# Bringing the solves' inverses back by 6 transfers instead of 12, with another split of heads over partitions

## The chip, the core and the metric

The kernel runs on one core of one Trainium2 chip. The metric is device time in microseconds (us) of one execution; lower is better.

## What is computed

The reference is one layer of a hybrid decoder. 256 tokens of width 2048 are normalised and projected once; half of the projected columns feed a sparse attention with 8 heads, the other half an RWKV-7 mixer with 16 heads of 64; both results are gated, projected out, normalised and added to the input. The change lies in the RWKV-7 part, whose core in the reference is a recurrence over tokens:

```python
def step(state, inp):
    r_t, w_t, k_t, v_t, a_t, b_t = inp
    sa = jnp.einsum('bhij,bhj->bhi', state, a_t)
    state = (state * w_t[:, :, None, :] + sa[..., None] * b_t[:, :, None, :]
             + v_t[..., None] * k_t[:, :, None, :])
    return state, jnp.einsum('bhij,bhj->bhi', state, r_t)
```

## The kernel before, in words

TensorE (PE) does almost all of the work: the input projection as a stream of weight tiles. A weight tile of 128 x 1024 (512 KB) is loaded by the SP queue into a raw buffer `rf__N` (line 281; four buffers), split by ScalarE (ACT) into a high part `hf__N` (line 289) and by VectorE (DVE) into a low part `lf__N` (line 290, called a cast here; three buffers), and multiplied with the activations `xH` and `xL` in 24 matmuls of 256 columns: 16 with `hf`, then 8 with `lf`. The last tiles of the stream, `ht`, `lt` and `ho`, `lo`, are of the same kind.

The rest of the layer is written as Python generators in "lanes". A planner steps them between the projection's pieces and gives each instruction a priority; from that, a scheduler puts every engine's instructions into one fixed order. At run time each engine follows its order and waits where an input is not there yet, so an instruction that waits holds up all that stands behind it on its engine.

The RWKV-7 recurrence is done in chunks of 64 tokens, in two halves of 8 heads (`hb` 0 and 1). For each half, `solve` (line 715) inverts 32 triangular 64 x 64 systems (8 heads, 4 chunks), each as two 32 x 32 diagonal blocks and one off-diagonal block:

1. Four transfers (line 726) take the diagonal blocks from the tile `GR` to a DRAM scratch `us`, and one (line 732) brings them back as 64 systems on 64 partitions, in `U`.
2. 62 VectorE instructions (lines 739 and 741) build the 64 inverses in `Z`, and line 744 copies the transposed inverses to `U`.
3. `Z` goes to the DRAM scratch `zs`, `U` to `zt` (lines 747 and 748, 256 KB each).
4. Eight transfers of 32 KB (line 761) bring the inverses back into the tile `ZB`, and four (line 768) the transposed ones of the first diagonal block into `ZT`. In traces both tiles are called `arena`, after the memory that they lie in; they are told apart by their source, `zs` or `zt`. Their runs of consecutive bytes are one row of 32 numbers, 128 bytes.
5. PE multiplies `GR` with `ZT` (32 matmuls of 32 x 32, lines 772 to 778; the first product from here on), VectorE copies it out (line 784), PE multiplies that with `ZB` (32 more, lines 789 to 796; the second product), and VectorE copies the off-diagonal blocks into `ZB` (line 799). A float32 matmul counts as two instructions in the profile.
6. The chunk loop (lines 808 to 884) runs four chunks one after the other through PE, ACT, VectorE and GpSimd (POOL).

A half has four feature tiles `i` of two heads each. Before, tile `i` worked on partition half `i % 2` in the steps 4 to 6; `i // 2` chose the columns there. This is why a read of one partition block needs tiles 0 and 2, or 1 and 3, which lie apart in the scratch, and takes two transfers:

```python
for a in range(2):
    SP.dma_start(ZBv[b0:b0 + 32, a, :, 32 * d:32 * d + 32], zsv[d, mp, :, a])
```

Of the kernel before, what the change touches and what calls it, by code (L numbers as in the profile page):

```python
# [16 lines left out]
P = 128  # L17
# [104 lines left out]
def hybrid_block(ctx: ExitStack, tc: tile.TileContext, xT, xtok, wfm, wtm, wout, vecs, gpost, lora, table,  # L122
                 onehot, consts, pos, cw1, cw2, out):
    nc = tc.nc
    PE, DVE, ACT, POOL, SP = nc.tensor, nc.vector, nc.scalar, nc.gpsimd, nc.sync
# [589 lines left out]
    def solve(hb):  # L715
# [3 lines left out]
        GR, AR, VS, KT, PC = A.GR, A.AR, A.VS, A.KT, A.PC  # L719
# [3 lines left out]
        for par in range(2):  # L723
            for d in range(2):
                b0 = 64 * (1 - par) + 32 * d
# [4 lines left out]
        U = Us.ap.rearrange("p (s t) -> p s t", s=32)[0:64]  # L730
# [13 lines left out]
        DVE.tensor_copy(U, Z.rearrange("p s t -> p t s"))  # L744
        zs = dp.tile([64, 32, 32], F32, tag="zs", name=f"zs{hb}")
        zt = dp.tile([64, 32, 32], F32, tag="zt", name=f"zt{hb}")
        SP.dma_start(zs, Z)
        SP.dma_start(zt, U)
        Us.free(3.0)
        Zs.free(3.0)  # L750
        ZBs = yield from sb(4)
        ZB = ZBs.ap.rearrange("p (j t) -> p j t", j=16)
        for mp in range(2):
            POOL.memset(ZB[64 * mp + 32:64 * mp + 64, :, 0:32], 0.0)
        zsv = zs.rearrange("(d a b k) s t -> d b s a k t", d=2, a=2, b=2)
        ZBv = ZB.rearrange("p (a k) t -> p a k t", a=2)
        for mp in range(2):
            for d in range(2):
                b0 = 64 * mp + 32 * d
                for a in range(2):  # L760
                    SP.dma_start(ZBv[b0:b0 + 32, a, :, 32 * d:32 * d + 32], zsv[d, mp, :, a])
        ZTs = yield from sb(2)
        ZT = ZTs.ap.rearrange("p (h a s) -> p h a s", h=8, a=2)
        ztv = zt.rearrange("(d h a b) t s -> d b t h a s", d=2, h=8, a=2)
        for par in range(2):
            b0 = 64 * (1 - par)
            for a in range(2):
                SP.dma_start(ZT[b0:b0 + 32, :, a, :], ztv[0, par, :, :, a])
        yield 11.0
        t2p = yield from bank2()  # L770
        t2v = t2p[:, :, 0:T].rearrange("p b (j a s) -> p b j a s", j=4, a=2)
        for i in range(4):
            for hh in range(2):
                for c in range(4):
                    b0 = 64 * (1 - c % 2)
                    q0 = 64 * (i % 2) + 32
                    mm(t2v[q0:q0 + 32, c % 2, 2 * (i // 2) + hh, c // 2, :], GR[b0:b0 + 32, i, hh, c, 32:64],
                       ZT[b0:b0 + 32, 2 * i + hh, c // 2, :], start=True, stop=True)
        t2s = yield from sb(2)
# [6 lines left out]
        ZTs.free(1.0)  # L786
        yield 2.0
        zbp = yield from bank()
        for i in range(4):
            for hh in range(2):  # L790
                for c in range(4):
                    q = 2 * (i // 2) + hh
                    j = 4 * q + c
                    q0 = 64 * (i % 2)
                    mm(zbp[q0:q0 + 32, j * 32:j * 32 + 32], t2[q0 + 32:q0 + 64, q, c // 2, c % 2, :],
                       ZB[q0 + 32:q0 + 64, j, 32:64], start=True, stop=True)
        for mp in range(2):
# [10 lines left out]
        for c in range(4):  # L808
            ko = 64 * (c % 2)
            bo = 64 - ko  # L810
            gps = yield from bank()
            for i in range(4):
                q0 = 64 * (i % 2)
                o_ = gps[q0:q0 + 64, (i // 2) * P:(i // 2) * P + P]
                for hh in range(2):
                    s = slice(64 * hh, 64 * hh + 64)
                    mm(o_[:, s], GR[:, i, hh, c, 0:64], VS[:, i, c, s], start=i < 2 and hh == 0,
                       stop=c == 0 and i >= 2 and hh == 1)
            if c:
                for i in range(4):  # L820
                    q0 = 64 * (i % 2)
                    o_ = gps[q0:q0 + 64, (i // 2) * P:(i // 2) * P + P]
                    mm(o_, AR[:, i, c, 0, :], SB.ap.rearrange("p (m t) -> p m t", m=4)[:, i, :], start=False,
                       stop=i >= 2)
            G = yield from sb()
            ACT.activation(G[:], gps[:, :T], AF.Copy)
            gps.free(2.0)
            yield GLAT
            sap = yield from bank2()
            for i in range(4):  # L830
                q0 = 64 * (i % 2)
                for hh in range(2):
                    o = (i // 2) * P + 64 * hh
                    mm(sap[bo:bo + 64, i % 2, o:o + 64], ZB[q0:q0 + 64, 8 * (i // 2) + 4 * hh + c, :],
                       G[q0:q0 + 64, o:o + 64], start=True, stop=True)
            DVE.tensor_copy(VS[bo:bo + 64, :, c, :].rearrange("p (a b) t -> p b a t", b=2),
                            sap[bo:bo + 64, :, 0:T].rearrange("p b (a t) -> p b a t", a=2))
            sap.free(2.0)
            G.free(1.0)
            yield GLAT  # L840
            SBo = SB
            if c < 3:
                sp = yield from bank()
                for i in range(4):
                    for hh in range(2):
                        s = slice(64 * hh, 64 * hh + 64)
                        mm(sp[s, i * 64:i * 64 + 64], KT[:, i, c, s], VS[:, i, c, s], start=True, stop=True)
                pcb = PC[:, :, c:c + 1].to_broadcast([P, 4, 64])
                S2 = yield from sb()
                S2v = S2.ap.rearrange("p (m t) -> p m t", m=4)  # L850
                spv = sp[:, :T].rearrange("p (m t) -> p m t", m=4)
                if c:
                    DVE.tensor_tensor(S2v, spv, SC.ap.rearrange("p (m t) -> p m t", m=4), op=ALU.add)
                    SC.free(1.0)
                else:
                    DVE.tensor_copy(S2v, spv)
# [12 lines left out]
            for i in range(4):  # L869
                o_ = yp[64 * (i % 2):64 * (i % 2) + 64, (i // 2) * P:(i // 2) * P + P]  # L870
                for hh in range(2):
                    s = slice(64 * hh, 64 * hh + 64)
                    mm(o_[:, s], GR[:, i, hh, c, 64:128], VS[:, i, c, s], start=i < 2 and hh == 0,
                       stop=c == 0 and i >= 2 and hh == 1)
            if c:
                for i in range(4):
                    o_ = yp[64 * (i % 2):64 * (i % 2) + 64, (i // 2) * P:(i // 2) * P + P]
                    mm(o_, AR[:, i, c, 1, :], SBo.ap.rearrange("p (m t) -> p m t", m=4)[:, i, :], start=False,
                       stop=i >= 2)
# [19 lines left out]
        for a in range(2):  # L899

            ytp = yield from bank()
            for c in range(4):
                o = T * c + P * a
                transpose(ytp[:, P * c:P * c + P], ysb[:, o:o + P], ident)
            ytv = ytp.ap.rearrange("p (c b t) -> p c b t", c=4, b=2)
            for b in range(2):
                m = 4 * hb + 2 * a + b
                mv = mix[1][:, m, :].rearrange("p (c t) -> p c t", c=4)
                DVE.scalar_tensor_tensor(mv, ytv[:, :, b, :], vcol(V_LNW, m), mv, op0=ALU.mult, op1=ALU.add)
            ytp.free(2.0)  # L910
            yield 0.5
# [493 lines left out]
```

## Time and profile before

| What | us |
|---|---|
| median of three runs | 571.77 |
| lowest and highest of them | 570.47, 571.91 |
| the profiled execution's own time | 571.67 |
| its span, from first to last instruction | 569.9 |
| PE busy in the span | 552.9 |
| VectorE busy | 427.1 |
| ScalarE busy | 311.1 |
| GpSimd busy | 56.3 |

The rows further down come from that one profiled execution, and their times count from the start of its span; 1.77 us of its own time lie outside the span. A matmul's duration in a row includes its pipeline, so matmuls overlap: what one costs in a stream is the distance of two starts.

### The profile page before, as it was taken

The numbers are of one execution on the slowest core, as the hardware profiler recorded it, in microseconds if no ns is written. First come the engines' busy times: TensorE is split into PE (matmuls) and PEld (weight loads), VectorE is DVE, ScalarE is ACT, GpSimd is POOL, SyncE is SP. The second block draws the span as 40 slices with busy tenths as digits, with TensorE's granted clock in tenths as the row PEclk, the third lists the DMA queues.
The fourth block names the chain that finished last, engine by engine and source line by source line (L and its number), as shares of the span: only waits on it lengthen the run. The fifth ranks groups of instructions, "written<-read, shape, count | busy, mean of one in ns | idle before, by whom it ended". The sixth has DMA issues, their size and how long they took to land.

```text
span 569.9 us, 12187 instructions
## 1 busy us (share of the span) xinstructions
PE 552.9 (97%) x4796; PEld 519.1 (91%) x4796; DVE 427.1 (75%) x892; ACT 311.1 (55%) x566; POOL 56.3 (10%) x95
## 2 busy tenths in 40 slices
PE   8999999999899989999999999999999999999994
PEld 8999999989899979999999999999999987778883
DVE  6888998866989955555798969998866664468755
ACT  6858864723346442332878856865633344465532
POOL 3101410510000000000402200000000010000002
PEclk9999999999999997999999999999999999999997
DMA  8857453578745572432364355344574436675623
GB/s 300 363 195 261 156 182 118 183 225 241 248 149 185 188 213 94 154 108 80 106 216 157 101 160 176 96 144 150 165 200 143 154 113 178 229 270 174 217 78 147
DMA packets 41364, 99.95 MB, mean 175 GB/s; under 512 B 14395, under 2 KB 17116, under 8 KB 40924
## 3 DMA queue, kind: packets, MB, share of 16 engines
q1 hardware_dynamic: 41020, 98.88, 53.4%
q8 instruction: 37, 0.61, 0.5%
q10 hardware_dynamic: 288, 0.31, 0.2%
q14 instruction: 19, 0.16, 0.1%
HBM read 93.93 MB, written 5.24 MB: 174 GB/s over the span
## 4 chain that ended last, share of the span: by engine, by line
PE 86%; DMA 5%; DVE 4%; ACT 2%; issue 1%; POOL 1%; SPq 1%; DVEq 0%; ACTq 0%; POOLq 0%
PE banks L156 84%; PE banks L169 2%; DMA arena<-zt 1%; DMA arena<-in_cw_dram 1%; DMA arena<-us 1%; DMA us<-GR 1%; DMA xr<-in_xT_dram 1%; POOL arena L629 1%; DVE y L1302 0%; DMA arena<-zs 0%; DVE arena L950 0%; SPq L726 0%; DVE arena L739 0%; DVE arena L631 0%; POOL arena L630 0%
## 5 line engine op out<-in xcount | busy, mean ns | idle before, releaser
L156 PE MATMUL banks<-arena 128*32 128x128 f32 (+3 forms) x470 | 30.4, 252 | 2.9 <-DMA arena<-in_cw_dram 1.8
L156 PEld LDWEIGHTS banks<-arena 128*32 128x32 f32 (+3 forms) x470 | 26.0, 135 | 6.4 <-DMA arena<-in_cw_dram 2.3
L739 DVE TENSOR_TENSOR arena<-arena 64x31 f32<-64x31 f32 (+15 forms) x62 | 20.4, 330 | 3.0 <-DMA arena<-us 2.4
L741 DVE TENSOR_TENSOR arena<-arena 64x31 f32<-64x31 f32 (+15 forms) x62 | 20.4, 329 | 0.5
L629 POOL TENSOR_SCALAR arena<-arena,small 128x256 f32<-128x256 f32 x8 | 9.6, 1196 | 92.0 <-ACT arena L627 91.7
L541 ACT ACTIVATE small<-small 128x256 f32<-128x256 f32 x25 | 12.3, 499 | 9.3 <-DVE small L539 9.3
L169 PE MATMUL banks<-small,arena 128*128 128x128 f32 x96 | 15.8, 275 | 0.8 <-DVE arena L656 0.5
L542 DVE SCALAR_TENSOR_TENSOR arena<-small 128x256 f32<-128x256 f32 x25 | 12.2, 491 | 4.1 <-ACT small L541 4.0
L156 PE MATMUL banks<-AR,arena 64*128 64x128 f32 x128 | 14.9, 287 | 0.3 <-ACT KT L665 0.3
L156 PEld LDWEIGHTS banks<-AR,arena 64*128 64x128 f32 x128 | 12.1, 187 | 2.5 <-issue 1.5
L596 DVE RECIPROCAL arena<-arena 128x256 f32<-128x256 f32 x8 | 13.8, 1736 | 0.5 <-ACT arena L593 0.5
L1049 ACT ACTIVATE arena<-arena,mx 128x256 f32<-128x256 f32 (+1 forms) x32 | 14.1, 443 | 0.0
L1107 ACT ACTIVATE arena<-arena 128x256 f32<-128x256 f32 x16 | 6.6, 412 | 13.0 <-DVE arena L1221 8.4
L169 PEld LDWEIGHTS banks<-small,arena 128*128 128x128 f32 x96 | 11.3, 140 | 1.9 <-DVE arena L656 0.7
L689 DVE TENSOR_TENSOR GR<-banks,small 128x1024 f32<-128x1024 f32 x8 | 9.8, 1221 | 3.4 <-ACT small L541 1.7
L1306 POOL TENSOR_TENSOR y<-y,xres 128x512 f32<-128x512 f32 x2 | 2.9, 1456 | 94.3 <-ACT y L1305 94.3
L156 PE MATMUL banks<-VS,GR 128*64 128x64 f32 x256 | 11.4, 228 | 0.0
L156 PEld LDWEIGHTS banks<-VS,GR 128*64 128x64 f32 x256 | 9.5, 137 | 2.0 <-DVE mixA L1119 0.4
L539 DVE TENSOR_TENSOR small<-banks,small 128x256 f32<-128x256 f32 x25 | 10.2, 414 | 0.1
L1045 DVE CUSTOM_DVE_ANT_0 arena<-banks,arena 128x256 f32<-128x256 f32 (+1 forms) x32 | 10.1, 348 | 0.0
L862 POOL MEMSET arena<- 64x256 f32 x12 | 3.7, 308 | 64.6 <-DVE arena L1108 36.5
L626 POOL TENSOR_SCALAR arena<-arena 128x256 f32<-128x256 f32 x8 | 8.1, 1013 | 17.6 <-ACT arena L625 17.5
(1375 smaller groups left out, 2148.1 us busy)
## 6 DMA issues: line engine op xcount, KB each, us to landing
arena<-in_cw_dram SPq DMA_DIRECT2D x8, 512.0 KB, 5.3
arena<-in_wfm_dram SPq DMA_DIRECT2D x4, 512.0 KB, 9.4
xres<-in_xtok_dram SPq DMA_DIRECT2D x2, 1024.0 KB, 6.4
xr<-in_xT_dram SPq DMA_DIRECT2D x3, 512.0 KB, 6.8
bscr<-arena SPq DMA_DIRECT2D x1, 1536.0 KB, 6.0
out_dram<-y SPq DMA_DIRECT2D x5, 256.0 KB, 2.3
arena<-bscr SPq DMA_DIRECT2D x8, 128.0 KB, 3.0
gpt<-in_gpost_dram SPq DMA_DIRECT2D x1, 1024.0 KB, 6.4
```

Of the source, the lines that this page charges most:

```text
L156: last[0] = PE.matmul(o, lhsT, rhs, **kw)
L169: PE.transpose(out=o, in_=i, identity=idn)
L539: DVE.tensor_tensor(f[:, 1:T + 1], pt[:, :T], rbc, op=ALU.mult)
L541: ACT.activation(tm, f[:, 0:T], AF.Copy, scale=vcol(V_MU, c))
L542: DVE.scalar_tensor_tensor(o, f[:, 1:T + 1], omu[:, c:c + 1], tm, op0=ALU.mult, op1=ALU.add)
L596: pace(DVE.reciprocal(A.nrm[i + j], A.nrm[i + j]))
L629: POOL.tensor_scalar(fk[:], ta[:], ka2[:, m:m + 1], ka1[:, m:m + 1], op0=ALU.mult, op1=ALU.add)
L689: DVE.tensor_tensor(A.GR[:, i].rearrange("p h c t -> p (h c) t"), gp.ap.rearrange("p h (c t) -> p (h c) t", c=4), gmask[:, None, :].to_bro ...
L739: DVE.tensor_tensor(t_, U[:, 0:j, j:j + 1].to_broadcast([64, j, w]), Z[:, j:j + 1, j:32].to_broadcast([64, j, w]), op=ALU.mult)
L741: DVE.tensor_tensor(Z[:, 0:j, j:32], Z[:, 0:j, j:32], t_, op=ALU.add)
L1045: DVE.tensor_tensor_reduce(out=dst, in0=src, in1=bb, scale=1.0, scalar=-3.0e38, op0=ALU.add, op1=ALU.max, accum_out=mx[:, i, j:j + 1])
L1049: ACT.activation(dst, dst, AF.Exp, bias=mx[:, i, j:j + 1], accum_out=sm[:, i, j:j + 1])
```

## The change

It does three things. The transposed inverses are written to DRAM first in the source, and their reads stand ahead of the others' in it. Feature tile `i` now works on partition half `i // 2`, and `i % 2` chooses the columns, so that a partition block's tiles lie side by side in the scratch: each pair of reads becomes one of 64 KB (four for `ZB`, two for `ZT`). The PE loops go over `i` in the order 0, 2, 1, 3, so that they alternate between partition halves as before; what is computed is the same. Lines after 770 have numbers that are smaller by 3 in the changed kernel.

```diff
+        SP.dma_start(zt, U)
         SP.dma_start(zs, Z)
-        SP.dma_start(zt, U)
         Us.free(3.0)
         Zs.free(3.0)
+        ZTs = yield from sb(2)
+        ZT = ZTs.ap.rearrange("p (h a s) -> p h a s", h=8, a=2)
+        ztv = zt.rearrange("(d r b) t s -> d b t r s", d=2, b=2)
+        for par in range(2):
+            b0 = 64 * (1 - par)
+            SP.dma_start(ZTs[b0:b0 + 32, :].rearrange("p (r s) -> p r s", r=16), ztv[0, par])
         ZBs = yield from sb(4)
         ZB = ZBs.ap.rearrange("p (j t) -> p j t", j=16)
...
-        zsv = zs.rearrange("(d a b k) s t -> d b s a k t", d=2, a=2, b=2)
-        ZBv = ZB.rearrange("p (a k) t -> p a k t", a=2)
+        zsv = zs.rearrange("(d b k) s t -> d b s k t", d=2, b=2)
         for mp in range(2):
             for d in range(2):
                 b0 = 64 * mp + 32 * d
-                for a in range(2):
-                    SP.dma_start(ZBv[b0:b0 + 32, a, :, 32 * d:32 * d + 32], zsv[d, mp, :, a])
-        ZTs = yield from sb(2)
-        ZT = ZTs.ap.rearrange("p (h a s) -> p h a s", h=8, a=2)
-        ztv = zt.rearrange("(d h a b) t s -> d b t h a s", d=2, h=8, a=2)
-        for par in range(2):
-            b0 = 64 * (1 - par)
-            for a in range(2):
-                SP.dma_start(ZT[b0:b0 + 32, :, a, :], ztv[0, par, :, :, a])
+                SP.dma_start(ZB[b0:b0 + 32, :, 32 * d:32 * d + 32], zsv[d, mp])
         yield 11.0
         t2p = yield from bank2()
         t2v = t2p[:, :, 0:T].rearrange("p b (j a s) -> p b j a s", j=4, a=2)
-        for i in range(4):
+        for i in (0, 2, 1, 3):
             for hh in range(2):
                 for c in range(4):
                     b0 = 64 * (1 - c % 2)
-                    q0 = 64 * (i % 2) + 32
-                    mm(t2v[q0:q0 + 32, c % 2, 2 * (i // 2) + hh, c // 2, :], GR[b0:b0 + 32, i, hh, c, 32:64],
+                    q0 = 64 * (i // 2) + 32
+                    mm(t2v[q0:q0 + 32, c % 2, 2 * (i % 2) + hh, c // 2, :], GR[b0:b0 + 32, i, hh, c, 32:64],
                        ZT[b0:b0 + 32, 2 * i + hh, c // 2, :], start=True, stop=True)
...
-            DVE.tensor_copy(VS[bo:bo + 64, :, c, :].rearrange("p (a b) t -> p b a t", b=2),
+            DVE.tensor_copy(VS[bo:bo + 64, :, c, :].rearrange("p (b a) t -> p b a t", b=2),
                             sap[bo:bo + 64, :, 0:T].rearrange("p b (a t) -> p b a t", a=2))
...
-                m = 4 * hb + 2 * a + b
+                m = 4 * hb + 2 * b + a
```

The other loops over `i` in the chunk loop are changed in the same way.

The scheduler makes a new order of it, which differs first in half 0's solve. On PE, in half 0 (the tile `GR_742` is half 0's), the first product's 32 matmuls stood inside the tile `hf__2436`; the row with `arena,GR_742` is that product, the one with `arena` alone the second.

```order
 L156 MATMUL banks<-xH,hf__2369 128x256
 L156 MATMUL banks<-xL,hf__2369 128x256
-L156 MATMUL banks<-xH,lf__2368 128x256 x8
+L156 MATMUL banks<-xH,lf__2368 128x256 x6
+L156 MATMUL banks<-arena,GR_742 32x32 x32
+L156 MATMUL banks<-xH,lf__2368 128x256 x2
 L156 MATMUL banks<-xH,hf__2404 128x256
```

```order
 L156 MATMUL banks<-xH,hf__2436 128x256
+L156 MATMUL banks<-arena 32x32 x32
 L156 MATMUL banks<-xL,hf__2436 128x256
 L156 MATMUL banks<-xH,hf__2436 128x256
-L156 MATMUL banks<-arena,GR_742 32x32
 L156 MATMUL banks<-xL,hf__2436 128x256
-L156 MATMUL banks<-arena,GR_742 32x32 x31
```

The first product now stands 35 projection matmuls earlier, behind the sixth matmul with `lf__2368`. The second product stands 36 earlier than it did (it stood inside `lf__2470`).

On the SP queue, the same place in half 0, before:

```order
L747 DMA zs_2531<-arena 64x1024
L748 DMA zt_2532<-arena 64x1024
L281 DMA rf__2500<-in_wfm_dram 128x1024
L761 DMA arena<-zs_2531 32x8x32 x4
L281 DMA rf__2552<-in_wfm_dram 128x1024
L761 DMA arena<-zs_2531 32x8x32 x4
L281 DMA rf__2582<-in_wfm_dram 128x1024
L768 DMA arena<-zt_2532 32x8x32 x4
```

and in the changed kernel, where `rf__2546` and `rf__2576` are the loads that were called `rf__2552` and `rf__2582`:

```order
L748 DMA zs_2531<-arena 64x1024
L747 DMA zt_2532<-arena 64x1024
L281 DMA rf__2500<-in_wfm_dram 128x1024
L765 DMA arena<-zs_2531 32x16x32 x2
L756 DMA arena<-zt_2532 32x16x32 x2
L281 DMA rf__2546<-in_wfm_dram 128x1024
L765 DMA arena<-zs_2531 32x16x32 x2
L281 DMA rf__2576<-in_wfm_dram 128x1024
```

The scheduler still writes `zs` first and puts two reads of `zs` ahead of the reads of `zt`; but no weight load stands between those and the reads of `zt` any more, where there were two.

On the SP queue in half 1, before:

```order
L747 DMA zs_5233<-arena 64x1024
L281 DMA rf__5202<-in_wfm_dram 128x1024
L748 DMA zt_5234<-arena 64x1024
L281 DMA rf__5253<-in_wfm_dram 128x1024
L761 DMA arena<-zs_5233 32x8x32 x8
L281 DMA rf__5284<-in_wfm_dram 128x1024
L768 DMA arena<-zt_5234 32x8x32 x4
```

and in the changed kernel, where `rf__5163`, `rf__5196`, `rf__5241` and `rf__5272` are the loads that were called `rf__5169`, `rf__5202`, `rf__5253` and `rf__5284`:

```order
L748 DMA zs_5227<-arena 64x1024
L747 DMA zt_5228<-arena 64x1024
L281 DMA rf__5163<-in_wfm_dram 128x1024
L756 DMA arena<-zt_5228 32x16x32 x2
L281 DMA rf__5196<-in_wfm_dram 128x1024
L281 DMA rf__5241<-in_wfm_dram 128x1024
L281 DMA rf__5272<-in_wfm_dram 128x1024
L765 DMA arena<-zs_5227 32x16x32 x4
```

Here the reads of `zt` come first, and the reads of `zs` now stand behind the load that they stood ahead of.

## Rows read from the trace of the kernel before

**Rows 1.** The page, busy time of the engines over the span.

```profile
PE 552.9 (97%) x4796; PEld 519.1 (91%) x4796; DVE 427.1 (75%) x892; ACT 311.1 (55%) x566; POOL 56.3 (10%) x95
```

**Rows 2.** Waits of PE: engine, line, awaited; us in total, times, longest.

```profile
PE banks L156 <- DMA arena<-zt: 2.8, 1, 2.8
PE banks L156 <- DMA arena<-in_cw_dram: 1.8, 2, 1.5
```

**Rows 3.** The chain that ended last, in order of time: start, us, what.

```profile
207.80 5.40 DMA arena<-zt
213.25 76.41 PE banks L156 x880
```

**Rows 4.** Stretches: length, then busy us by engine, granted clock, DMA share, GB/s.

```profile
210.46:213.25 2.79, 0.00 (x1) 0.01 (x1) 0.94 (x2) 0.51 (x1) 0.00 (x0) 0.88 1.02 237
213.25:221.20 7.95, 7.95 (x98) 7.52 (x98) 3.23 (x6) 1.20 (x2) 0.00 (x0) 0.61 0.24 82
423.15:428.64 5.49, 5.49 (x99) 5.15 (x98) 3.27 (x7) 1.28 (x2) 0.00 (x0) 1.00 0.50 159
```

**Rows 5.** The same view, around PE's wait for in_cw_dram.

```profile
145.00:150.00 5.00, 3.78 (x56) 3.37 (x54) 4.90 (x12) 1.93 (x4) 1.03 (x2) 1.00 0.82 275
```

**Rows 6.** Timeline of the SP queue in half 0: start, us, queue, line, transfer.

```profile
198.59 0.46 SPq L748 DMA_DIRECT2D zt<-arena  x1
...
202.54 1.81 SPq L761 DMA_DIRECT2D arena<-zs  x4
204.45 0.39 SPq L281 DMA_DIRECT2D rf__2552<-in_wfm_dram  x1
...
207.80 1.91 SPq L768 DMA_DIRECT2D arena<-zt  x4
```

**Rows 7.** DMA issues by stretch, 197 to 210 us: KB each, median us to landing.

```profile
zt<-arena SPq DMA_DIRECT2D x1, 256.0 KB, 4.5
...
arena<-zs SPq DMA_DIRECT2D x4, 32.0 KB, 2.0
...
arena<-zs SPq DMA_DIRECT2D x4, 32.0 KB, 3.6
...
arena<-zt SPq DMA_DIRECT2D x4, 32.0 KB, 4.9
```

**Rows 8.** Line 726 (the 64 KB transfers us<-GR, both halves): issue to landing.

```profile
DMA to landing us min/median/max: 1.7/1.9/5.3
```

**Rows 9.** Timeline of PE in half 0: start, us, matmul, count, idle before and why.

```profile
205.38 1.12 PE L156 MATMUL banks<-xH,lf__2368 128*128 128x256 f32 x8
206.34 0.28 PE L156 MATMUL banks<-xH,hf__2404 128*128 128x256 f32 x1
...
213.25 0.31 PE L156 MATMUL banks<-arena,GR 32*32 32x32 f32 x2 [2.79 <-DMA arena<-zt]
```

**Rows 10.** Timeline of VectorE in half 0.

```profile
208.31 0.48 DVE L542 SCALAR_TENSOR_TENSOR arena<-small 128x256 f32<-128x256 f32 x1 [0.64 <-ACT small L541]
...
215.41 1.56 DVE L784 COPY arena<-banks 32x256 f32<-32x256 f32 x4 [4.01 <-PE banks L156]
```

**Rows 11.** Timeline of VectorE at the end of half 1's solve.

```profile
402.56 1.21 DVE L290 TENSOR_TENSOR lf__4993<-rf__4991,hf__4994 128x1024 fp32r<-128x1024 f32 x1
...
409.46 1.12 DVE L744 COPY arena<-arena 64x1024 f32<-64x1024 f32 x1
...
416.18 1.23 DVE L290 TENSOR_TENSOR lf__5137<-rf__5135,hf__5138 128x1024 fp32r<-128x1024 f32 x1 [0.27 <-PE banks L156]
```

**Rows 12.** Timeline of PE in half 1.

```profile
415.02 1.12 PE L156 MATMUL banks<-xH,lf__5035 128*128 128x256 f32 x8
...
423.15 0.24 PE L156 MATMUL banks<-arena,GR 32*32 32x32 f32 x2
```

**Rows 13.** DMA issues by stretch, 407 to 421 us, as in rows 7.

```profile
zt<-arena SPq DMA_DIRECT2D x1, 256.0 KB, 6.3
...
arena<-zt SPq DMA_DIRECT2D x4, 32.0 KB, 2.9
```

More of the change, by code (lines that the diff above doesn't have):

```diff
@@ L788, in solve @@
         zbp = yield from bank()
-        for i in range(4):
+        for i in (0, 2, 1, 3):
             for hh in range(2):
                 for c in range(4):
-                    q = 2 * (i // 2) + hh
+                    q = 2 * (i % 2) + hh
                     j = 4 * q + c
-                    q0 = 64 * (i % 2)
+                    q0 = 64 * (i // 2)
                     mm(zbp[q0:q0 + 32, j * 32:j * 32 + 32], t2[q0 + 32:q0 + 64, q, c // 2, c % 2, :],
@@ L811, in solve @@
             gps = yield from bank()
-            for i in range(4):
-                q0 = 64 * (i % 2)
-                o_ = gps[q0:q0 + 64, (i // 2) * P:(i // 2) * P + P]
+            for i in (0, 2, 1, 3):
+                q0 = 64 * (i // 2)
+                o_ = gps[q0:q0 + 64, (i % 2) * P:(i % 2) * P + P]
                 for hh in range(2):
                     s = slice(64 * hh, 64 * hh + 64)
-                    mm(o_[:, s], GR[:, i, hh, c, 0:64], VS[:, i, c, s], start=i < 2 and hh == 0,
-                       stop=c == 0 and i >= 2 and hh == 1)
+                    mm(o_[:, s], GR[:, i, hh, c, 0:64], VS[:, i, c, s], start=i % 2 == 0 and hh == 0,
+                       stop=c == 0 and i % 2 == 1 and hh == 1)
             if c:
-                for i in range(4):
-                    q0 = 64 * (i % 2)
-                    o_ = gps[q0:q0 + 64, (i // 2) * P:(i // 2) * P + P]
+                for i in (0, 2, 1, 3):
+                    q0 = 64 * (i // 2)
+                    o_ = gps[q0:q0 + 64, (i % 2) * P:(i % 2) * P + P]
                     mm(o_, AR[:, i, c, 0, :], SB.ap.rearrange("p (m t) -> p m t", m=4)[:, i, :], start=False,
-                       stop=i >= 2)
+                       stop=i % 2 == 1)
             G = yield from sb()
@@ L829, in solve @@
             sap = yield from bank2()
-            for i in range(4):
-                q0 = 64 * (i % 2)
+            for i in (0, 2, 1, 3):
+                q0 = 64 * (i // 2)
                 for hh in range(2):
-                    o = (i // 2) * P + 64 * hh
-                    mm(sap[bo:bo + 64, i % 2, o:o + 64], ZB[q0:q0 + 64, 8 * (i // 2) + 4 * hh + c, :],
+                    o = (i % 2) * P + 64 * hh
+                    mm(sap[bo:bo + 64, i // 2, o:o + 64], ZB[q0:q0 + 64, 8 * (i % 2) + 4 * hh + c, :],
                        G[q0:q0 + 64, o:o + 64], start=True, stop=True)
-            DVE.tensor_copy(VS[bo:bo + 64, :, c, :].rearrange("p (a b) t -> p b a t", b=2),
+            DVE.tensor_copy(VS[bo:bo + 64, :, c, :].rearrange("p (b a) t -> p b a t", b=2),
                             sap[bo:bo + 64, :, 0:T].rearrange("p b (a t) -> p b a t", a=2))
@@ L843, in solve @@
                 sp = yield from bank()
-                for i in range(4):
+                for i in (0, 2, 1, 3):
                     for hh in range(2):
@@ L868, in solve @@
             yp = yield from bank()
-            for i in range(4):
-                o_ = yp[64 * (i % 2):64 * (i % 2) + 64, (i // 2) * P:(i // 2) * P + P]
+            for i in (0, 2, 1, 3):
+                o_ = yp[64 * (i // 2):64 * (i // 2) + 64, (i % 2) * P:(i % 2) * P + P]
                 for hh in range(2):
                     s = slice(64 * hh, 64 * hh + 64)
-                    mm(o_[:, s], GR[:, i, hh, c, 64:128], VS[:, i, c, s], start=i < 2 and hh == 0,
-                       stop=c == 0 and i >= 2 and hh == 1)
+                    mm(o_[:, s], GR[:, i, hh, c, 64:128], VS[:, i, c, s], start=i % 2 == 0 and hh == 0,
+                       stop=c == 0 and i % 2 == 1 and hh == 1)
             if c:
-                for i in range(4):
-                    o_ = yp[64 * (i % 2):64 * (i % 2) + 64, (i // 2) * P:(i // 2) * P + P]
+                for i in (0, 2, 1, 3):
+                    o_ = yp[64 * (i // 2):64 * (i // 2) + 64, (i % 2) * P:(i % 2) * P + P]
                     mm(o_, AR[:, i, c, 1, :], SBo.ap.rearrange("p (m t) -> p m t", m=4)[:, i, :], start=False,
-                       stop=i >= 2)
+                       stop=i % 2 == 1)
             ACT.activation(ysb[:, T * c:T * c + T], yp[:, :T], AF.Copy)
```

## The prediction

> **What bounds the kernel now.** I read the page's busy times first. PE is busy for 97% of the span [rows 1], so the time is PE's work plus the moments in which PE stands still or runs slowly; work saved on another engine or queue gives nothing by itself. Next I read who PE waits for. The longest single wait is 2.8 us on the reads of `zt`, once; the next is 1.5 us on `in_cw_dram` [rows 2]. The chain of waits confirms that this one counts: it runs through a transfer issued at 207.80 and goes on with PE's first product at 213.25 [rows 3]. So the wait lies in half 0's solve. Half 1's first product, at 423.15, shows no wait [rows 12].
>
> Then I asked what the stop costs beyond its own length. Three stretches show it [rows 4]. In the first, the stop itself, PE does nothing for 2.79 us. In the second, from the first product to the start of the second one, the same work as in the third, which is half 1's, takes 7.95 us instead of 5.49. The granted clock is the reason: a mean of 0.61 in the second, 1.00 in the third, so that for most of it PE ran at 1.2 GHz and not at 2.4. The stop came just before, and the clock fell during it (0.88). The slow stretch costs 7.95 - 5.49 = 2.46 us, and the whole event 2.79 + 2.46 = **5.25 us**.
>
> Why were the reads late? On the SP queue [rows 6], the write of `zt` went out at 198.59 and landed 4.5 us later [rows 7], at 203.1. Its reads were issued only at 207.80, because eight reads of `zs` and two weight loads of 512 KB stood ahead of them; and they took 4.9 us to land, where the first four reads of `zs`, with no weight load just ahead, took 2.0, and the next four, behind `rf__2552`, 3.6 [rows 7].
>
> **The change, part by part.**
>
> *The reads of `zt` move forward in half 0.* In the new order two reads of `zs`, of 64 KB, and then the two of `zt` follow on `rf__2500`, without a weight load between. Four issues took 1.81 us, 0.45 each [rows 6]. So from 202.54 the `zs` pair takes until 203.44, and the reads of `zt` go out at 203.44 and 203.90; the write of `zt`, landed at 203.1, does not hold them. How long does a 64 KB transfer with 128-byte runs take to land? The nearest below are the 64 KB transfers of line 726 with the same runs, 1.7 at the least and 1.9 in the middle [rows 8]; the first four reads of `zs` took 2.0 at the same place on the queue; the far end is 5.3, the longest of line 726. I take 2.0, because those transfers had the same load ahead of them. Then `ZT` is there at 205.4 and 205.9.
>
> *The first product moves forward on PE.* It now stands behind the sixth matmul with `lf__2368`. Eight of these take from 205.38 to 206.34 [rows 9], 0.12 us each, so PE gets there at 205.38 + 6 x 0.12 = 206.10. Both reads have landed, with 0.2 us to spare: no stop, and by the same reckoning no fall of the clock. This is the whole gain: -2.79 - 2.46.
>
> *What is late next in half 0.* The first product costs 5.49 - 34 x 0.12 = 1.41 us at the full clock (34 projection matmuls lie in that stretch of half 1). The second product stands 33 matmuls behind it: 206.10 + 1.41 + 33 x 0.12 = 211.5. It needs the copies of line 784, which now stand right behind line 542 and ahead of two casts; line 542 starts at 208.31 and takes 0.48, the copies 1.56 [rows 10], so they end at 210.35, 1.1 us early. It needs the last two reads of `zs`, issued behind `rf__2546` by 205.3; with 3.6 us to landing they are there at 208.9. The two casts slip by 1.6 us, and serve matmuls that come some 4 us and more later. In the chunk loop the distances on PE between dependent steps are those of before, but for one that shrinks from 34 projection matmuls to 26, a distance that the next chunk had before without a wait. I cost all of this at nothing.
>
> *Half 1.* Nothing can be gained here, only lost. The copy of line 744 now stands two casts earlier, shortly behind the counterpart of `lf__4993`, which ends at 403.8 [rows 11]; so it starts at about 404.5 instead of 409.46, and `zt` is written from 405.6. That write lands in 4.5 to 6.3 us [rows 7, 13], by 411.9, and the first read in 2.9 to 4.9 more, between 413.0 and 416.8. PE reaches the first sixteen matmuls two projection matmuls behind the counterpart of `lf__5035`: 415.02 + 10 x 0.12 = 416.2 [rows 12]. So the loss is nothing to 0.6 us; the middle says nothing. The reads of `zs` now follow `rf__5272`, whose raw buffer is freed by the counterpart of `lf__5137`, at 417.4 [rows 11]. They go out by 419.2 and land by 422.8 to 424.1; PE needs them at 423.15 + 1.41 = 424.6. Nothing lost here either.
>
> *The removed transfers and the other edits.* Six issues less per half save SP 6 x 0.45 = 2.7 us in each, time in which SP mostly waits for a buffer; the loads behind them go out a little earlier, on which PE never waited here. The bytes are the same. The order of the loops over `i`, the pattern of VectorE's copy into `VS` and the tile number `m` change no count and no size. Zero.
>
> **The sum.** From the profiled execution: 571.67 - 2.79 - 2.46 = **566.4 us**. That execution lies 0.1 below the median of the runs shown, so it can stand for them.
>
> **A rule that speaks against it.** The four first reads of `zs` moved 32 KB each, the new ones move 64 KB with the same 128-byte runs; [rows 8] shows such transfers landing no later than the small ones. The Trainium skill, "DMA: Bandwidth & Descriptors", section "Specifications", asks for at least 512 B to move at line rate and says that shorter pieces cost a read-modify-write; by it, joining two reads without lengthening their runs saves no moving time. No run here shows what 512-byte runs would do. What it would mean here is the first rival.
>
> **The rivals.**
>
> 1. *Double the bytes, double the landing.* If a 64 KB read needs twice the 2.0 us, the second read of `zt` lands at 203.90 + 4.0 = 207.9 and PE stops for 1.8 us. A stop of 1.5 left the clock at 1.00 [rows 2, 5], one of 2.79 did not. With the clock kept: 568.2; with the fall: 570.7. For it: the transfers share the queue with two others of 64 KB. Against it: [rows 8].
> 2. *A stop that takes the place of the old one (slower).* PE now arrives at the first product 4.2 us earlier than before, so a read that lands late costs more than it did. The point that decides is a landing at 206.10 + 2.79 = 208.9: later than that, the change loses. If the write of `zt` took 6.3 us as in half 1 [rows 13], the reads would go out at 204.9 and 205.3, and with the longest landing of rows 8 they would be there at 210.6: a stop of 4.5 us and the slow stretch, 566.4 + 4.5 + 2.5 = 573.4. Against it: the queue ahead of these reads is the same as before up to 203.4.
> 3. *A new stop elsewhere.* From here on the scheduler's order differs on every engine, since half 0 ends 40 projection matmuls earlier and half 1 begins earlier. A new wait of the size of the one on `in_cw_dram`, 1.5 to 1.8 us [rows 2], would give 568.0 to 568.2, one that also costs the clock about 571. Against it: the dependent steps stand about as far apart as before.
> 4. *The change does not do what it says.* It half does not: in half 0 the scheduler still writes and reads `zs` first. The prices above are for the order as it is; transposed reads first would have 0.9 us more to spare. It has no chance of its own.
>
> **How the numbers follow.** A measurement of this kernel tells about 0.3%, 1.7 us, from no change. The forecast has a chance of 0.62. Rival 1 has 0.15, a third of it with the clock's fall; rival 3 has 0.13, about half of it with the fall; rival 2 has 0.07; 0.03 is left for no change at all from causes not seen. Faster by over 0.3% (below 570.1) is the forecast, 0.10 of rival 1 and 0.07 of rival 3: 0.79. Within 0.3% are the rest of these and the 0.03: 0.14. Slower: 0.07. The range ends at the bottom 1.3 below the forecast, as far as the lowest run shown lies below the median, 565.1; at the top it takes in rival 1 with the clock's fall, 570.8.
>
> **What would show it.** PE's wait on `arena<-zt` should be gone, or below 0.5 us; the granted clock between PE's start and its end should stay at 1.00; the reads of `zt` should be issued near 203.5 and land near 205.9; the distance from first to second product in half 0 should be 5.4 to 5.5 us, as in half 1. A wait of PE on `zt` of 1.5 us or more, or a new one elsewhere, a fallen clock near 206 us, or a time above 570 would show the forecast wrong.

## The result, and the profile after

The change took the kernel from 571.49 us (median, 570.47 to 571.91) to 566.89 us (566.66 to 567.37): a ratio of 0.992, 95% interval 0.991 to 0.994. The profiled execution took 566.86 us, its span fell from 569.9 to 565.1 us. The forecast was 566.4.

The page of the changed kernel, busy times and the row of PE's clock:

```profile
PE 552.0 (98%) x4796; PEld 517.8 (92%) x4796; DVE 428.1 (76%) x892; ACT 311.9 (55%) x566; POOL 56.9 (10%) x95
...
PEclk9999999999999999999999999999999999999998
```

PE still sets the end, with the same 4796 matmuls. The wait on `zt` that headed PE's waits in [rows 2] is in none of its waits now:

```profile
PE banks L156 <- POOL arena L271: 1.1, 1, 1.1
PE banks L156 <- DMA arena<-in_cw_dram: 0.8, 2, 0.4
PE banks L169 <- DVE arena L656: 0.5, 1, 0.5
PE banks L156 <- DVE lo__6142 L290: 0.5, 1, 0.5
PE banks L156 <- ACT small L1149: 0.5, 1, 0.5
```

The SP queue in half 0 (start, us, line, transfer), to be laid beside [rows 6]:

```profile
198.09 0.45 SPq L747 DMA_DIRECT2D zt<-arena  x1
199.26 0.33 SPq L281 DMA_DIRECT2D rf__2500<-in_wfm_dram  x1
201.35 0.86 SPq L765 DMA_DIRECT2D arena<-zs  x2
202.30 0.97 SPq L756 DMA_DIRECT2D arena<-zt  x2
203.37 0.44 SPq L281 DMA_DIRECT2D rf__2546<-in_wfm_dram  x1
203.85 0.95 SPq L765 DMA_DIRECT2D arena<-zs  x2
```

The reads of `zt` go out at 202.30 and about 202.8, ahead of the next weight load and 5.5 us earlier than before. How long they take (DMA issues from 195 to 212 us; KB each, median us to landing):

```profile
zt<-arena SPq DMA_DIRECT2D x1, 256.0 KB, 3.8
arena<-zs SPq DMA_DIRECT2D x4, 64.0 KB, 3.5
arena<-zt SPq DMA_DIRECT2D x2, 64.0 KB, 2.2
```

So `ZT` is there by 202.8 + 2.2 = 205.0. PE arrives 0.7 us later and goes on without a gap (timeline of PE):

```profile
204.89 0.88 PE L156 MATMUL banks<-xH,lf__2368 128*128 128x256 f32 x6
205.70 1.01 PE L156 MATMUL banks<-arena,GR 32*32 32x32 f32 x64
206.64 0.50 PE L156 MATMUL banks<-xH,lf__2368 128*128 128x256 f32 x2
```

The stretches before the first product, and from it to the second (length, busy time by engine, granted clock, DMA share, GB/s), answer to the first two of [rows 4]:

```profile
195.00:205.70 10.70, 10.70 (x90) 10.57 (x89) 7.71 (x14) 5.31 (x7) 1.01 (x2) 1.00 0.82 229
205.70:210.78 5.08, 5.08 (x99) 4.90 (x98) 4.35 (x9) 2.52 (x3) 0.00 (x0) 1.00 0.62 181
```

The clock stays at 1.00, 2.4 GHz, and the way from product to product takes 5.08 us where it took 7.95. The span's 4.8 us are then: 2.79 of the stop, 2.87 of the slow stretch, and 0.5 by which PE was already ahead when it came to `lf__2368` (204.89 above, 205.38 in [rows 9]); against these stand about 1.0 us of small waits, the new ones (0.5 on line 1149 above, three of 0.2 to 0.3) less one of 0.3 that vanished; together 5.2. The 0.5 is chance, since both kernels have the same order up to there: PE waited 1.0 less on `in_cw_dram` (0.8 for 1.8) and 0.9 less on `xH` near the start, and other instructions of that part started later. The 0.4 us by which that is too much I did not place.

### The profile page after: what moved, and what is told of

Same layout as the page of the kernel before. It is cut to its first block, busy times and chain, and to the rows that moved or that the text cites. A ratio compares the mean times of both kernels' runs of the same rounds, so it can differ in the third digit from the quotient of the medians.

```text
span 565.1 us, 12166 instructions
## 1 busy us (share of the span) xinstructions
PE 552.0 (98%) x4796; PEld 517.8 (92%) x4796; DVE 428.1 (76%) x892; ACT 311.9 (55%) x566; POOL 56.9 (10%) x95
## 4 chain that ended last, share of the span: by engine, by line
PE 83%; DVE 6%; DMA 4%; ACT 2%; POOL 2%; issue 2%; SPq 1%; DVEq 0%; ACTq 0%; POOLq 0%
PE banks L156 81%; PE banks L169 2%; DMA xr<-in_xT_dram 1%; POOL arena L629 1%; DMA arena<-us 1%; DMA arena<-in_cw_dram 1%; DMA us<-GR 1%; DMA rt__3408<-in_wtm_dram 1%; SPq L726 0%; DVE y L1299 0%; DVE arena L631 0%; POOL arena L630 0%; DVE arena L947 0%; POOL arena L626 0%; SPq L327 0%
## 5 line engine op out<-in xcount | busy, mean ns | idle before, releaser
L574 ACT ACTIVATE hr<-arena 128x256 fp32r<-128x256 f32 x16 | 6.6, 415 | 7.6 <-DVE arena L677 5.7
L653 POOL COPY AR<-arena 128x4 f32<-128x4 f32 x8 | 5.7, 713 | 38.4 <-DVE arena L643 38.4
```

## The experiments

All times are medians; each ratio is to runs of the kernel before on the same chip, with a 95% interval. The queue theory says: the reads of `zt` were late because weight loads stood ahead of them on SP, and the gain is PE's stop with its slow stretch. Its rivals put the gain in the number of transfers, in the source's order, or in the new place of the heads.

| kernel | time, us | ratio | PE's stops on `zt` in half 0, us, in the one profile |
|---|---|---|---|
| order alone | 569.36 | 0.9991 (0.9972 to 1.001) | none |
| merging and heads alone | 574.66 | 1.0065 (1.0042 to 1.0087) | none |
| the change, all reads split | 569.9 | 1.0007 (0.9984 to 1.003) | 0.94 + 0.97 |
| before, `zt` read by ACT | 569.14 | 0.9988 (0.9961 to 1.0015) | none |
| the change again | 567.87 | 0.9953 (0.9929 to 0.9976) | none |
| the change, `zt` read by ACT | 568.25 | 0.994 (0.992 to 0.9959) | none |
| the change, reads of `zs` split | 568.53 | 0.9959 (0.9941 to 0.9977) | none |
| before, priority of `zt` alone | 570.2 | 0.9982 (0.9962 to 1.0003) | none |
| reads of `zt` late, 512 | 581.07 | 1.0207 (1.0155 to 1.0259) | 9.6 |
| reads of `zt` late, 1024 | 587.19 | 1.0305 (1.0263 to 1.0347) | 16.7 |
| reads of `zt` late, 2048 | 596.83 | 1.0471 (1.0426 to 1.0516) | 20.0 + 3.1 |
| the change, two `in_cw` loads by ACT | 568.07 | 0.9936 (0.9913 to 0.9959) | 0.97 |

### The order alone

```
-        SP.dma_start(zs, Z)
         SP.dma_start(zt, U)
+        SP.dma_start(zs, Z)
...
+        (the four reads of zt, as before, ahead of the eight of zs)
```

> The kernel before with the order alone changed (the write and the reads of zt stand first in the source, still 12 transfers of 32 KB, heads as before). On SP in half 0 two reads of zt now stand ahead of rf__2552 and two behind it, on PE the first product moves forward as in the change. Queue theory (what counts is that every read of zt is issued ahead of the next 512 KB load and lands before PE comes): the third and fourth read go out at about 204.9 and 205.4 and land 3.6 to 4.9 us later, at 208.5 to 210.3, PE is there at about 206.0: a stop of 2.5 to 4.3 us, the clock falls as before, 571 to 573 us, ratio 1.000 to 1.003. Rival (transposed reads first is what brings the gain): no stop, 566.5 to 567 us, ratio 0.992.

Inconclusive. The profiled execution took 567.91 us without a stop: the third read, issued behind `rf__2552` at 203.47, landed after 3.1 us, not 3.6 to 4.9, just ahead of PE (206.62). The median is not shown to differ from before. With no spare left, the runs go up to 572.9.

### The merging and the heads' place alone

```
-        SP.dma_start(zt, U)
         SP.dma_start(zs, Z)
+        SP.dma_start(zt, U)
...
-        (the two reads of zt ahead of the four of zs)
+        (the four reads of zs ahead of the two of zt)
```

> The change without its order: 6 transfers of 64 KB and the new place of the heads, but zs is written and read first in the source. On SP in half 0 the reads of zt stand behind four of zs and rf__2546; on PE the first product stands 20 projection matmuls behind its place in the change. Queue theory: reads issued at 204.9 and 205.4, landing 3.6 to 4.9 us later at 208.5 to 210.3, PE is there at 208.5: a stop of 0 to 1.8 us, the clock stays up to 1.5: 566.5 to 568.2 us, ratio 0.991 to 0.994. Rival (the order is what brings the gain, fewer transfers bring nothing): the stop stays as before, 571.5, ratio 1.000.

A miss of both sides: slower than before, by 0.4 to 0.9%. In half 0 the queue theory held: PE met the first product at 208.62 with no stop and took 5.07 us to the second. The time was lost later, in waits of PE that neither theory had:

```profile
PE banks L156 <- ACT small L1149: 2.1, 1, 2.1
...
PE banks L169 <- ACT arena L1065: 1.0, 1, 1.0
PE banks L156 <- DVE GR L689: 0.9, 1, 0.9
```

Half 0's second product came at 213.69 where the change has it at 210.78, and ACT's order around line 1149 differs; that the one set off the other is argued, not shown. Two stretches of this kernel (260 to 310 and 310 to 400 us) show what it costs:

```profile
260.00:310.00 50.00, 47.87 (x399) 46.81 (x398) 39.53 (x87) 34.52 (x69) 6.18 (x11) 0.97 0.45 140
310.00:400.00 90.00, 87.35 (x703) 84.44 (x702) 77.14 (x276) 58.13 (x157) 11.50 (x17) 1.00 0.39 131
```

PE does nothing for 2.1 and 2.7 us in them, in the change for 0.5 and 0.6; that and the clock of 0.97 are over half of the 8 us between this profiled execution (575.3) and those of the change (566.9 and 567.3). The clock fell behind the stop of 2.13 us that ended at 286.00; the 4 us from there had a mean of 0.57, which costs 4.00 x 0.43 = 1.7 us:

```profile
286.00:290.00 4.00, 4.00 (x20) 4.00 (x21) 3.22 (x9) 1.52 (x3) 0.00 (x0) 0.57 0.46 155
```

This is the prediction's third rival, a new stop elsewhere, met in a neighbour of the change.

### The change with all its reads split

```
+            for r in (0, 8):   (two reads of 8 heads for each one of zt)
...
+                for k in (0, 8):   (and of zs)
```

> The change with each of its reads cut in two along the heads: order and place of the heads as in the change, but 12 transfers of 32 KB. SP's order in half 0 is that of the kernel with the order alone. Queue theory: the second half of the zt reads goes out behind rf__2552 and lands at 208.5 to 210.3, PE is there at about 206: a stop of 2.5 to 4.3 us, 571 to 573 us, ratio 1.000 to 1.003. Rival (the heads' new place, or the order, brings the gain): 566.5 to 567, ratio 0.992.

The queue theory, in its kind: the pair behind `rf__2552` landed after 3.0 and 4.5 us, too late. PE's timeline:

```profile
207.26 0.43 PE L156 MATMUL banks<-arena,GR 32*32 32x32 f32 x8 [0.94 <-DMA arena<-zt]
...
209.22 1.11 PE L156 MATMUL banks<-arena,GR 32*32 32x32 f32 x24 [0.97 <-DMA arena<-zt]
```

and its stretches, from the first product to the second:

```profile
204.76:207.26 2.50, 1.57 (x35) 1.25 (x34) 2.25 (x4) 0.42 (x2) 0.17 (x1) 1.00 0.96 263
207.26:209.22 1.96, 0.98 (x12) 0.74 (x12) 1.33 (x3) 1.30 (x2) 0.00 (x0) 0.84 0.71 192
209.22:215.95 6.73, 6.73 (x52) 6.53 (x52) 2.07 (x3) 1.06 (x1) 0.00 (x0) 0.54 0.42 122
```

11.19 us where the change takes 5.08: 1.91 of stops, about 3.1 of clock (6.73 x 0.46) and some 1.1 more; the first product runs in three pieces here, which may be the reason. The profiled execution took 572.94 us. Other runs of the same kernel took as little as 568.1, with a clock of 0.996, so the late landing hardly comes each time: the median, 569.9, lies below the 571 to 573 expected, and is not shown to be faster than before. The heads' place and the source's order were both in this kernel: by themselves they do not bring the gain.

### The kernel before, its reads of `zt` issued by ACT

```
-                SP.dma_start(ZT[b0:b0 + 32, :, a, :], ztv[0, par, :, :, a])
+                ACT.dma_start(ZT[b0:b0 + 32, :, a, :], ztv[0, par, :, :, a])
```

> The kernel before with the four reads of zt issued by ACT instead of SP, nothing else: 12 transfers of 32 KB, zs first. On ACT a pair of them stands ahead of the cast to hf__2471 and a pair behind it; on PE the first product stands where it does in the change, spread over some 12 projection matmuls. Queue theory (the reads were late because of what stood ahead of them on SP): issued as soon as zt is written, 203.1, they land by 205.2, the second pair a cast of about 1 us later by 206.3, PE is there at 205.5 to 206.9: a stop of 0 to 0.8 us, no fall of the clock, 566.5 to 567.5 us, ratio 0.991 to 0.993. Rival (size and number of the reads matter, or PE meets them 4 us too early): a stop of 2 us or more, 570 us or more, ratio above 0.997.

The profile has no stop, but the time is a miss of the theory: 569.14 us and 0.9988 lie above its ranges, the ratio's interval holds 1, three of the twelve runs have clocks of 0.991 or less, and one of these took 576 us. Issued by ACT, the first two reads landed in 2.1 us, where the median of the four was 4.9 before. The third went out at 203.90, 0.1 us behind the weight load `rf__2552` on SP, and took 3.9 (DMA issues from 202.9 to 203.5 and from 203.85 to 204.0 us; the landing of the fourth is not in the trace):

```profile
arena<-zt ACTq DMA_DIRECT2D x2, 32.0 KB, 2.1
...
arena<-zt ACTq DMA_DIRECT2D x1, 32.0 KB, 3.9
```

So by this trace a weight load issued just ahead makes a read late from the other queue too; it is the order of issue that counts, not SP as such. PE met no stop because its order brought it to the last reads' half of the product only at 208.20.

### The change again, and with `zt` on ACT, or `zs` split

The first is the changed kernel itself; the edits of the other two are

```
-            SP.dma_start(ZTs[...
+            ACT.dma_start(ZTs[...
```

and

```
-                SP.dma_start(ZB[b0:b0 + 32, :, 32 * d:32 * d + 32], zsv[d, mp])
+                for k in (0, 8):
+                    SP.dma_start(ZB[b0:b0 + 32, k:k + 8, 32 * d:32 * d + 32], zsv[d, mp, :, k:k + 8])
```

> The changed kernel itself once more, beside many more runs of the kernel before. In the last four experiments the 30 runs of the kernel before spread from 567.1 to 572.8 us, with mean granted clocks from 0.997 down to 0.989. Theory (the event, a late landing of zt, comes in part of the runs of the kernel before and never in the change): every run of the change keeps a clock of 0.993 or more and lies at 566.5 to 568.5 us, those of before spread as they did, ratio 0.993 to 0.997. Rival 1 (the event of 5.25 us is in every run of before and is always gone): ratio 0.990 to 0.993. Rival 2 (the change has late landings of its own, as the run with split reads had): runs of the change at 571 us and above with clocks of 0.991 or less, ratio 0.997 to 1.000.

> The change with its two reads of zt issued by ACT; PE's order is exactly that of the change. It gives the reads more spare (none of zs ahead of them; issued as soon as ACT gets to them, about 203). Theory (the reads of the change land in time already): no stop at the first product, the same time as the change within 1 us, 566.5 to 568.5, ratio 0.993 to 0.997. Rival (the change has too little spare and loses in some runs): fewer slow runs than the change, a median 1 us or more below it.

> The change with only its reads of zs cut in two again: 2 reads of zt of 64 KB, 8 of zs of 32 KB, 10 in all. On SP the reads of zt stand where they do in the change, ahead of the next weight load; on PE the first product comes three matmuls earlier. Theory (all that counts is that both reads of zt stand ahead of that load): no stop or one below 0.5 us, 566.5 to 569 us, ratio 0.993 to 0.998, the time of the change. Rival (the number of transfers counts): between the change and the kernel with all reads split, ratio 0.998 to 1.001.

These ran beside each other. The change is faster again, by less than the first time: 0.9953. Seven of its nine runs lie at 567.0 to 568.9 with clocks of 0.995 or more, six of them within the theory's range; two, at 569.1 and 570.7 with 0.992, have clocks that it did not allow. Moving the reads to ACT with PE's order kept changes nothing that can be told (0.994), nor does splitting the reads of `zs` (0.9959, ten transfers for six). So the number of transfers does not count; the reads of `zt` as two ahead of the next load are enough. Beside it stands the kernel with all reads split, which has the same heads and source order but two of its four reads of `zt` behind that load: 1.0007.

### The kernel before, with the priority of `zt`'s reads raised

```
+                with at("fetch"):
                     SP.dma_start(ZT[b0:b0 + 32, :, a, :], ztv[0, par, :, :, a])
```

> The kernel before with the scheduler's priority of its four reads of zt raised to that of the weight loads, nothing else: 12 transfers, heads as before, zs written first. On SP two reads of zs, then all four of zt stand ahead of rf__2552; on PE the first product comes 5 matmuls earlier than in the change. Theory (place on the queue alone counts): four issues of 0.45 us behind two of zs, from 202.3 to 204.1, the last landing 2.0 to 2.4 us later at 206.3, PE is there at about 205.3: a stop of 0 to 1.2 us, below the 1.5 us that left the clock alone, 567 to 569 us, ratio 0.994 to 0.998. Rival (merging or the heads' new place is needed): a stop of 2 us or more with the clock's fall, ratio 1.000 or more.

No stop in the profiled execution, which took 567.61 us, but the median is 570.2, above the range, and 8 of 12 runs have a clock below 0.995. Four issues take 1.88 us, two take 0.97: the last read lands at about 205.7, and PE comes at 205.79. If other executions missed that 0.1 us, which no trace shows, this is the use of merging: not fewer transfers, but two issues less between the write of `zt` and the end of its reads.

### Reads made late on purpose

These are the change with `zt` on ACT and one thing more: ahead of the reads of `zt`, on ACT's queue, stands a transfer of n x 32 single numbers (n = 16, 32, 64). PE's order is the same in all three.

```
+        if hb == 0:
+            dq = dp.tile([32, n], F32, tag="dq", name="dq")
+            ACT.dma_start(dq, zt[0:n, 0, :].rearrange("a b -> b a"))
```

> The change with its reads of zt issued by ACT, and ahead of them, in half 0 alone, one more transfer on ACT's queue: 512 single numbers of 4 B from zt to an unused place. It changes nothing that is computed. The order on PE is the same in this kernel and in the two with 1024 and 2048 numbers (the first product four projection matmuls later than in the change, with one between its halves), so the three differ only in how late the reads of zt land. No row shows what such a transfer takes; I put it at 2 us for 512, 4 for 1024, 8 for 2048, an estimate from the transfers of line 761 (1024 pieces in about 2 us). Theory (a late landing costs its stop and, from about 2 us, the clock's fall): the last read lands at about 207.5, PE is there at about 207.5 to 208: a stop of 0 to 0.5 us, 567 to 569 us. Rival (PE's stops are made up later, the event costs nothing by itself): all three kernels within 1 us of each other.

> As the kernel with 512 numbers, with 1024: the reads of zt land about 2 us later. Theory: a stop of 1.5 to 2.5 us, with a fall of the clock if it is above 2: 1.5 to 5 us more than with 512, 569 to 573 us. Rival (made up later): the time with 512. Second rival (the clock's fall has nothing to do with the stop): just the stop more, and a clock of 1.00 behind it.

> As the kernel with 512 numbers, with 2048: the reads of zt land about 6 us later. Theory: a stop of 5 to 7 us and a slow stretch of about 2.5 us behind it, 7 to 10 us more than with 512, 575 to 578 us, the granted clock at its lower level in some 5 us behind the stop. Rival (made up later): the time with 512. Second rival (stop alone): 5 to 7 us more and the clock at 1.00.

The extra transfer took 9.0, 16.4 and 23.2 us, three to four and a half times my estimate (last section), so the doses are far larger than expected. As a series they are the better for it. PE's wait in the three, one fence each:

```profile
PE banks L156 <- DMA arena<-zt: 9.6, 1, 9.6
```

```profile
PE banks L156 <- DMA arena<-zt: 16.7, 1, 16.7
```

```profile
PE banks L156 <- DMA arena<-zt: 23.1, 2, 20.0
```

And the stretch from the first product to the second (33 projection matmuls between them, as in the change; in the third kernel 3.1 us of it are a second stop):

```profile
216.48:224.78 8.30, 8.30 (x98) 7.82 (x98) 2.85 (x5) 1.06 (x1) 0.00 (x0) 0.65 0.14 54
```

```profile
222.96:232.44 9.48, 9.48 (x98) 8.99 (x98) 3.13 (x6) 1.06 (x1) 0.00 (x0) 0.55 0.03 13
```

```profile
226.69:239.28 12.59, 9.49 (x97) 8.94 (x97) 3.08 (x6) 1.06 (x1) 0.00 (x0) 0.54 0.18 57
```

In the change with `zt` on ACT, the kernel without the extra transfer, this stretch is

```profile
207.07:212.49 5.42, 5.42 (x99) 5.22 (x98) 4.69 (x9) 2.52 (x3) 0.00 (x0) 1.00 0.47 152
```

Take the stop and what the stretch has above 5.42 off each profiled execution: 580.67 - 9.60 - 2.88 = 568.2; 588.45 - 16.73 - 4.06 = 567.7; 595.11 - 23.06 - 4.07 = 568.0. The kernel without the delay takes 568.2. Nothing of a stop is made up later, and the sum that the prediction was built on, stop plus slow stretch, holds to 0.5 us over stops of 0 to 23, in one execution of each. Both rivals fall: the times are not equal, and the clock is low behind each stop. Its price does not follow the stop's length: 2.9, 4.1 and 4.1 us.

### Two loads of `in_cw_dram` on ACT

PE's next wait has the same look, loads behind weight loads; so I tried the same cure there.

```
-            pace(SP.dma_start(cws[n][:], cw1...
+            pace((ACT if n in (4, 6) else SP).dma_start(cws[n][:], cw1...
```

> The change with two of the eight loads of in_cw_dram (the fifth and the seventh) issued by ACT; the order on PE and on VectorE is exactly that of the change. PE's stops on in_cw_dram took 0.8 us in the first profile of the change and 2.4 in the second, 0.3 to 0.6 near 133 us and 0.3 to 1.8 near 150. Theory (the same reason as that of the change: these loads wait behind weight loads on SP): both stops gone, 0.8 to 2.4 us less than the change, 565.5 to 567.0 us beside its 566.9 and 567.9, ratio 0.989 to 0.993. Rival (ACT issues the seventh load at 146.1, no earlier than SP at 145.0 to 145.7, and it shares the engines with the weight load anyway): the stops stay, the time of the change, 567 to 568.5, ratio 0.993 to 0.997.

The rival: 568.07 us, the time of the change. PE's waits:

```profile
PE banks L156 <- DMA arena<-in_cw_dram: 1.8, 2, 1.3
...
PE banks L156 <- DMA arena<-zt: 1.0, 1, 1.0
```

ACT issued the seventh load at 144.81, SP at 145.67 in the first profile of the change and 145.02 in the second: hardly earlier. The Trainium skill, "DMA: Bandwidth & Descriptors", section "Issuing engines are not separate DMA queues", says that issuing from another engine saves only the time on the sequencer; here the stops stayed, which agrees. No version beat the change.

## Why the prediction was right, point by point

**The event as the whole gain.** Right, and the late reads show it best: stop and slow stretch add up to the time. In the change both are gone. That the forecast met the profiled time to 0.5 us is in part luck: the event was worth 5.66 rather than 5.25, 0.5 came by chance ahead of it, and about 1.0 of small waits, put at nothing, went off again.

**How much of it.** Right in the first comparison, where 4.6 of 5.25 us came; less in the second, 3.5 between medians. A reason shows in the 75 runs of the kernel before beside the experiments: 22 have a mean granted clock of 0.990 or less and a median of 572.5 us, 15 have 0.995 or more and 568.6, the rest lie between. The profile of before, at 0.989, was of the first kind. The clock also falls near the end of each profile (in the change the last slice of the clock's row): with no other fall the means are 0.995 (the priority alone) to 0.997 (the change). A stretch of 6 us at half clock takes off 0.005 more, so runs of the second kind can hardly have had the slow stretch; they lie 3.9 us below the first kind, and 1.7 and 0.7 us above the two medians of the change. The medians of the kernel before go from 568.7 to 571.9 in the four sets of runs, so the gain depends on which executions it is measured against. That the event makes the difference is argued, not shown: only one execution of the kernel before has a trace. And three kernels without a stop on `zt` in their profiles (the order alone, `zt` by ACT, the priority alone) are not shown to be faster than before; what their other executions met stays open. What the prediction did not ask is how often its one profiled execution is met.

**When the reads go out and land.** Forecast 203.44 and 203.90 with 2.0 us to landing; it was 202.30 and 202.8 with 2.2, all of half 0 being 0.5 to 1.1 us earlier in this execution. In other profiles of this order the two took 3.1 and 3.0 us (the change again) and 2.5 and 3.5 (with the `in_cw` loads on ACT), where reads of 32 KB with no weight load just ahead took 1.8 to 2.4. So the first rival's late landing came in part; that the size is the reason is not shown. In the change again the weight load ahead, `rf__2500`, landed only at 205.2, in the first profile at 203.7, and the reads 0.6 to 1.3 us behind it in both. With the 3.5 us PE stopped for 0.97 us, half the rival's 1.8, with the clock kept; the forecast's spare of 0.2 is as thin as it looked.

**What is late next in half 0.** Right: forecast a product-to-product distance of 5.5 us; it was 5.08, since the first product runs as one piece here (1.12 us by the same reckoning, not 1.41). The copies, now line 781, end at 209.2, 1.6 us ahead of PE; forecast 1.1. VectorE then waits for PE, not PE for it:

```profile
207.63 1.56 DVE L781 COPY arena<-banks 32x256 f32<-32x256 f32 x4
...
212.72 1.38 DVE L796 COPY arena<-banks 32x512 f32<-32x512 f32 x2 [0.69 <-PE banks L156]
```

**Half 1.** No loss, as forecast, with more spare than I gave it: `zt` was written from 399.42 and its reads went out at 403.00, landing after 3.3 us; PE came at 409.22. I had the write at 405.6; 5 of the 6 us are what the kernel had gained by then.

**The removed transfers at zero.** Right: ten transfers do as well as six. Merging is worth something by the place that it gives the reads of `zt`: with heads and source order kept, four of them gave 1.0007 and two 0.9959, each against the kernel before on its own chip. That I did not count.

**A stop of 1.5 us keeps the clock, one of 2.79 does not.** Too simple. It held for the change again (1.76 us on `in_cw_dram`, clock 1.00 before and after it), but a stop of 2.13 us brought a fall too (merging and heads alone), and so did two of 0.94 and 0.97 us with small matmuls and little else between them.

**The other rivals.** A read landing after 208.9, the slower side, did not come in the change; made on purpose it costs what the rival said, stop and slow stretch. The new stop elsewhere came in the change only as waits of 0.2 to 0.5 us, and in full in its neighbour without the source's order.

## What to carry to other kernels

Where an engine without slack stops for a small transfer, look at what is issued ahead of that transfer, on its queue and on the other, and count the issues of its own group too: cutting them to what fits before the next large load was worth more here than the transfers saved. Price a stop of TensorE as its length plus the slow stretch behind it, and read both from windows. Before you trust a gain taken from one profile, see whether the other executions of the old kernel show the event at all; and where a scheduler orders the rest, allow for new waits from the new order: merging alone lost half a per cent with them.

## What the hardware showed that was not expected

A transfer of single numbers of 4 B is very slow and slows the rest. DMA issues from 200 to 215 us in the kernels with 512, 1024 and 2048 of them:

```profile
rf__2548<-in_wfm_dram SPq DMA_DIRECT2D x1, 512.0 KB, 12.4
...
dq<-zt ACTq DMA_DIRECT2D x1, 2.0 KB, 9.0
```

```profile
rf__2548<-in_wfm_dram SPq DMA_DIRECT2D x1, 512.0 KB, 20.4
...
dq<-zt ACTq DMA_DIRECT2D x1, 4.0 KB, 16.4
```

```profile
rf__2548<-in_wfm_dram SPq DMA_DIRECT2D x1, 512.0 KB, 22.3
...
dq<-zt ACTq DMA_DIRECT2D x1, 8.0 KB, 23.2
```

2 KB took 9.0 us and 4 KB 16.4, 16 to 18 ns for each number; 8 KB took 23.2, 11 ns. The 64 KB reads of line 756 in the change, 512 pieces of 128 B, took 2.2. And a weight load on the other queue, 4.0 us in the change, took 12.4 to 22.3 beside it: another queue is no shelter.

The price of the clock's fall came out between 1.7 and 4.1 us in six profiles, and it does not follow the length of the stop: 1.7 behind 2.13 us, 2.5 to 2.9 behind 2.79, about 3.1 behind 0.94 and 0.97, 2.9 behind 9.6, and 4.1 behind 16.7 and behind 20.0 and 3.1. It is near half the time that PE then works at the lower clock: in the three late kernels 8.30 x 0.35 = 2.9, 9.48 x 0.45 = 4.3, and 12.59 x 0.46 less half of the second stop, 4.2. Two short stops can pay as much as one of 9.6 us.
